# Half of an output projection as seven products of halves, with the weights' sums made by adding DMAs

## The chip, the cores and the metric

The kernel runs on one core of a Trainium2 chip. The metric is the device time of one execution in microseconds. Engines are named as in the profile: PE is TensorE (PEld its weight loads), DVE is VectorE, ACT is ScalarE, POOL is GpSimd and SP is SyncE, which issues most of the DMAs.

## The reference

One layer of a bidirectional encoder on 256 tokens of width 2048, all in float32:

```
x -> x + RMSNorm_post( W_out( sum_b sigmoid(g_b(xn)) * P_b( branch_b(xn) * silu(gate_b(xn)) ) ) )
xn = RMSNorm_pre(x)
```

The branches are a bidirectional gated linear recurrence and a windowed attention with 16 heads. What matters here is the end:

```python
merged = (jax.nn.sigmoid(m_lru) * (y_a @ w_proj_a[l])
          + jax.nn.sigmoid(m_attn) * (y_b @ w_proj_b[l]))
x = x + rms_norm(merged @ w_out[l], norm_post_w[l])
```

`merged` is 256 x 2048 and `w_out` 2048 x 2048. The output projection `merged @ w_out` is the part that the change touches.

## The kernel before

All weights stream through the core once, in the order of a list that `load_plan` writes. Each entry is a load of 1 MiB into a tile `raw` (128 x 2048). A "blk" entry is 128 columns of a matrix over all 2048 rows; a "quad" entry is 512 columns over a quarter of the rows. Two entries after one another for "blk", four for "quad", make one output tile.

The kernel computes in two parts: a float32 operand is split into a rounded high part (type fp32r) and the remainder, and a product is the sum of three matmuls (`mm3`: high by high, high by low, low by high). Weights are split in halves of a load: `split(q)` makes `wh` with a cast on ACT and `wl` with a subtraction on DVE (`parts_of`). The rings are three deep for `raw` and five deep for `wh` and `wl`.

The order of the work is written out by hand. `steps` holds one function for each entry of the plan, and the loop at the end of `body` walks through the half steps `hs`: at the first half of step `i` it issues the load of step `i + 3` on SP (`fetch`); at each half it runs what is due at that half (`due`, filled by `at` and `soon`), then splits the weights for four halves later, then issues the half's matmuls on PE. Each engine runs its own instructions in this order.

The last stages are these. For each of four column blocks `c`, `add_pb` gives `w_proj_b`'s product; its `done` multiplies with the gate and adds the other branch into `sm[c]` (DVE, four operations of 128 x 512). In the two half steps after it, `turn` transposes two blocks of 128 columns on PE into a PSUM bank (`mt`) and splits them into `ms`, the projection's left operand, with tokens in the free dimension. Then comes the projection: for each `c` four quad steps in `add_rows`, 24 matmuls each, 12 in each half, with two PSUM tiles for the tokens 0 to 127 and 128 to 255. `o_evac` squares the result on ACT (`junk`), multiplies it by the norm's weight on DVE (`yw`), and with the last block forms the scale and the output and stores it.

For the last block (`last`) the matmuls of tokens 128 to 255 of its last two steps are held back, so that the first 128 tokens are evacuated and stored beside them.

PSUM has eight banks: tag "bg" has four single banks (`bank`), tag "mm" two pairs (`banks`). The projection's blocks were all taken from "bg" (`spare=True`), one tile for each token block. `load_tail` loads the post norm's weight (`npt`, 2 x 512 KB) and the rows of `x` for the residual (`xr`, 4 x 512 KB) when the projection starts; the tiles come from a pool of 31 units of 4 KB per partition.

Of the kernel before, what the change touches and what calls it, by code (L numbers as in the profile page):

```python
# [27 lines left out]
EPS = 1e-6  # L28
# [14 lines left out]
       ("w_proj_a", 1536), ("w_in", MA0), ("w_in", MA0 + 512)]  # L43


PV_NORM = 0
PV_CW = 16
PV_CB = PV_CW + 64
# [7 lines left out]
def load_plan():  # L56

    plan = []

    def quad(m, c):  # L60
        plan.extend(("quad", m, c, i) for i in range(4))

    def pair(m, c, n):
        plan.extend(("blk", m, c + (n + i) * P, 0) for i in range(2))

    quad("w_in", U0)
    for i in range(8):
# [19 lines left out]
    for c in range(4):  # L87
        quad("w_out", c * 512)
    return plan


def body(ctx, tc, x, xT, wall, wlru, pvec, npost, ident_d, mask_d, rope_d, out):
    nc = tc.nc
# [3 lines left out]
    small = ctx.enter_context(tc.tile_pool(name="small", bufs=2))  # L97
# [3 lines left out]
    def unit(name, dt=F32, shape=(P, 4, S)):  # L101
        return units.tile(list(shape), dt, tag="u", name=name)
# [17 lines left out]
    def parts_of(h, l, src, cast=nc.scalar.copy):  # L120
        cast(h, src)  # L121
        nc.vector.tensor_tensor(l, src, h.bitcast(F32), ALU.subtract)  # L122
# [4 lines left out]
    plan = load_plan()  # L127
# [3 lines left out]
    def at(hs, fn):  # L131
        assert hs >= now[0], (hs, now[0])
        due.setdefault(hs, []).append(fn)
# [7 lines left out]
        at(now[0] + d, fn)  # L141


    raws, parts = {}, {}

    def fetch(i):
        if i >= len(plan) or i in raws:
            return
        raws[i] = ring.tile([P, 2048], F32, tag="raw", name=f"raw{i}", bufs=3)
        nc.sync.dma_start(raws[i], wall[i])  # L150

    def split(q, c=0, w=1024, cast=nc.scalar.copy):
        i, h = q // 2, q % 2
        if i >= len(plan):
            return
        if c == 0:
            parts[q] = [ring.tile([P, 1024], F32R, tag=f"w{s}", name=f"w{s}{i}_{h}", bufs=5) for s in "hl"]
        wh, wl = parts[q]
        parts_of(wh[:, c:c + w], wl[:, c:c + w], raws[i][:, h * 1024 + c:h * 1024 + c + w], cast)

    def mm3(ps, wh, wl, xh, xl, start, stop):
        nc.tensor.matmul(ps, wh, xh, start=start, stop=False)  # L162
# [38 lines left out]
    def add_rows(name, act, done, spare=False, last=False):  # L201


        got, held = [], []

        def products(t, g, h, wh, wl):
            ts = slice(t * P, (t + 1) * P)
            for j in range(2):
                k = 4 * g + 2 * h + j
                sl = slice(j * 512, (j + 1) * 512)  # L210
                a = act[k // 2][:, k % 2, :, ts]
                mm3(got[t], a[:, 0], a[:, 1], wh[:, sl], wl[:, sl], k == 0, k == KT - 1)

        def half(g, h, wh, wl):
            if g == 0 and h == 0:
                if spare:
                    got.extend(bank(f"{name}{t}", (P, 512)) for t in range(2))
                else:
                    ps = banks(name, (P, 2, 512))
                    got.extend(ps[:, t] for t in range(2))  # L220
            products(0, g, h, wh, wl)
            if last and g >= 2:
                held.append((1, g, h, wh, wl))
            else:
                products(1, g, h, wh, wl)
            if g == 3 and h == 1:
                if last:
                    done(0, got[0])
                    for a in held:
                        products(*a)  # L230
                    done(1, got[1])
                else:
                    soon(lambda: [done(t, got[t]) for t in range(2)])

        for g in range(4):
            steps.append(("quad", lambda h, wh, wl, g=g: half(g, h, wh, wl)))


    warm = const.tile([P, 1], F32, name="warm")
# [262 lines left out]
            nc.vector.tensor_tensor(dst, dst, sg, ALU.mult)  # L502
        return done

    tm, sm, ms = [], [], []


    def gate_evac(units_list, c):
# [146 lines left out]
    def add_pb(c):  # L655
        def done(t, ps):
            g = sm[c][:, t]
            nc.vector.tensor_tensor(g, ps, g, ALU.mult)
            nc.vector.tensor_tensor(g, tm[c][:, t], g, ALU.add)
            if t == 1:  # L660
                for i in range(2):
                    soon(lambda i=i: turn(i), i + 1)

        def turn(i):

            ps = bank(f"mt{c}{i}")
            for j in range(2):
                sl = slice((2 * i + j) * P, (2 * i + j + 1) * P)
                for t in range(2):
                    nc.tensor.transpose(ps[:, j, t * P:(t + 1) * P], sm[c][:, t, sl], ident)  # L670
# [25 lines left out]

    def load_tail():
        for h in range(2):
            sl = slice(h * 1024, (h + 1) * 1024)
            npt.append(unit(f"np{h}", F32, (P, 1024)))  # L700
            nc.sync.dma_start(npt[h], npost[:, sl])
            for t in range(2):
                xr[t].append(unit(f"xr{t}{h}", F32, (P, 1024)))
                yw[t].append(unit(f"yw{t}{h}", F32, (P, 1024)))
                nc.sync.dma_start(xr[t][h], x[t * P:(t + 1) * P, sl])

    at(2 * len(steps) + 2, load_tail)

    def o_evac(c):
        def done(t, ps):  # L710
            cs = slice((c % 2) * 512, (c % 2 + 1) * 512)
            junk = small.tile([P, 512], F32, tag="p", name=f"junk{c}{t}", bufs=2)
            sums, bb = so[t], bias[t]
            nc.scalar.activation(junk, ps, AF.Square, accum_out=sums[:, c:c + 1])
            if c == 3:
                nc.scalar.activation(bb, sums[:, 3:4], AF.Sqrt, scale=1.0 / D, bias=bb)
            nc.vector.tensor_tensor(yw[t][c // 2][:, cs], ps, npt[c // 2][:, cs], ALU.mult)
            if c == 2:
                nc.vector.tensor_tensor(sums[:, 0:1], sums[:, 0:1], sums[:, 1:2], ALU.add)
                nc.vector.tensor_tensor(sums[:, 0:1], sums[:, 0:1], sums[:, 2:3], ALU.add)  # L720
                nc.vector.tensor_scalar(bb, sums[:, 0:1], 1.0 / D, EPS, ALU.mult, ALU.add)
                if t == 1:
                    nc.scalar.activation(warm, eps, AF.Sqrt)
            if c == 3:
                nc.vector.reciprocal(bb, bb)
                for q in range(4):
                    cs = slice((q % 2) * 512, (q % 2 + 1) * 512)
                    y = yw[t][q // 2][:, cs]
                    nc.vector.scalar_tensor_tensor(y, y, bb, xr[t][q // 2][:, cs], ALU.mult, ALU.add)
                    eng = nc.sync if q % 2 == 0 else nc.scalar  # L730
                    eng.dma_start(out[t * P:(t + 1) * P, q * 512:(q + 1) * 512], y)
        return done

    for c in range(4):
# [25 lines left out]

def pack_weights(w):
    loads = []
    for kind, m, c, i in load_plan():
        if kind == "quad":
# [58 lines left out]
```

## Time and profile before

| | |
|---|---|
| time, median of 3 runs | 921.52 us (920.87 to 921.70) |
| the profiled execution's own time | 921.43 us |
| its span | 919.6 us |
| granted TensorE clock, mean | 0.998 |
| the projection's matmuls | 384, from 823.8 to 912.2 us of the span |
| DMA in the whole span | 172.30 MB, mean 187 GB/s |

The span runs from the first to the last instruction of the profiled execution; the time has 1.8 us more around it. A row of the groups names the line, the engine, the operation, the tiles written and read, the shape and the count, then the busy time in us and the mean of one in ns, then the engine's idle time just before these instructions and what ended it. A row of the timeline gives start, duration and operation. A row of the windows gives a stretch, its length, and each engine's busy time in it with the number of instructions, then the granted clock, the share of the 16 DMA engines that was busy, and the rate. PE's durations overlap, since matmuls are pipelined.

### The profile page before, as it was taken

How to read it: one execution, taken by the hardware profiler on the slowest of the kernel's cores; microseconds unless marked ns; L12 is line 12 of the kernel's file. 1: busy time of each engine (PE TensorE's matmuls, PEld its weight loads, DVE VectorE, ACT ScalarE, POOL GpSimd, SP SyncE). 2: the span in 40 equal slices, each digit the busy share in tenths (PEclk: the TensorE clock that was granted, in tenths of full speed). 3: DMA queues.
4: the chain of work that ended last, by engine and by line, in shares of the span. 5: the costliest groups of instructions: out<-in, count | busy, mean ns of one | idle time of the engine just before them, and what ended most of it. 6: DMA issues, size and time to landing. Idle time of an engine off the chain costs nothing.

```text
span 919.6 us, 13623 instructions
## 1 busy us (share of the span) xinstructions
PE 910.3 (99%) x5526; PEld 816.2 (89%) x5526; DVE 636.5 (69%) x877; ACT 525.4 (57%) x721; POOL 1.4 (0%) x23
## 2 busy tenths in 40 slices
PE   9999999999999999999999999999999999999996
PEld 8899999999999999888888888888888888888885
DVE  6976858596869788887686869665564555565554
ACT  7678576857487867854554544654464444344451
POOL 0000000000000000000000000000000000000000
PEclk9999999999999999999999999999999999999999
DMA  9765555445455364555444453544555555558532
GB/s 329 261 232 172 178 201 184 165 179 206 144 223 190 137 228 158 183 183 196 176 177 159 163 184 138 184 143 177 183 183 186 184 199 186 205 183 321 184 138 91
DMA packets 27615, 172.30 MB, mean 187 GB/s; under 512 B 3072, under 2 KB 3840, under 8 KB 8480
## 3 DMA queue, kind: packets, MB, share of 16 engines
q1 hardware_dynamic: 26832, 170.27, 52.0%
q10 hardware_dynamic: 720, 1.16, 0.4%
q8 instruction: 43, 0.70, 0.3%
q14 instruction: 20, 0.16, 0.0%
HBM read 169.32 MB, written 2.10 MB: 186 GB/s over the span
## 4 chain that ended last, share of the span: by engine, by line
PE 98%; DMA 1%; DVE 0%; ACT 0%; SPq 0%; DVEq 0%; issue 0%
PE q L186 6%; PE o L164 4%; PE o L162 4%; PE o L163 4%; PE ga L162 3%; PE gl L162 3%; PE gl L164 3%; PE ga L164 3%; PE ga L163 3%; PE gl L163 3%; PE q L185 3%; PE u L162 3%; PE u L164 3%; PE u L163 3%; PE u_ps L349 2%; PE k L162 1%
## 5 line engine op out<-in xcount | busy, mean ns | idle before, releaser
L122 DVE TENSOR_TENSOR wl<-raw,wh 128x1024 fp32r<-128x1024 f32 (+1 forms) x306 | 370.7, 1215 | 224.6 <-ACT wh L121 224.1
L121 ACT CAST wh<-raw 128x1024 fp32r<-128x1024 f32 (+1 forms) x305 | 316.5, 1044 | 239.6 <-PE o L164 33.1
L186 PE MATMUL q<-xs,wh 128*128 128x512 f32 x256 | 89.7, 396 | 0.0
L164 PE MATMUL gl<-xs,wl 128*128 128x256 f32 x256 | 72.5, 283 | 0.0
L164 PE MATMUL ga<-xs,wl 128*128 128x256 f32 x256 | 72.5, 283 | 0.0
L162 PE MATMUL ga<-xs,wh 128*128 128x256 f32 x256 | 72.5, 283 | 0.0
L162 PE MATMUL gl<-xs,wh 128*128 128x256 f32 x256 | 72.4, 283 | 0.0
L163 PE MATMUL gl<-xs,wh 128*128 128x256 f32 x256 | 72.4, 283 | 0.0
L163 PE MATMUL ga<-xs,wh 128*128 128x256 f32 x256 | 72.4, 283 | 0.0
L185 PE MATMUL q<-xs,wl 128*128 128x256 f32 x240 | 67.0, 279 | 0.0
L186 PEld LDWEIGHTS q<-xs,wh 128*128 128x128 f32 x256 | 47.3, 188 | 9.9
L164 PE MATMUL u<-xs,wl 128*128 128x256 f32 x192 | 54.4, 283 | 0.0
L162 PE MATMUL u<-xs,wh 128*128 128x256 f32 x192 | 54.3, 283 | 0.0
L163 PE MATMUL u<-xs,wh 128*128 128x256 f32 x192 | 54.3, 283 | 0.0
L162 PE MATMUL o<-wh,ms 128*128 128x512 f32 x128 | 50.0, 390 | 0.0
L164 PE MATMUL o<-wh,ms 128*128 128x512 f32 x128 | 49.8, 389 | 0.0
L163 PE MATMUL o<-wl,ms 128*128 128x512 f32 x128 | 49.8, 389 | 0.0
L162 PEld LDWEIGHTS gl<-xs,wh 128*128 128x128 f32 x256 | 49.1, 192 | 0.1
L163 PEld LDWEIGHTS gl<-xs,wh 128*128 128x128 f32 x256 | 49.1, 192 | 0.1
L162 PEld LDWEIGHTS ga<-xs,wh 128*128 128x128 f32 x256 | 49.1, 192 | 0.0
L163 PEld LDWEIGHTS ga<-xs,wh 128*128 128x128 f32 x256 | 49.1, 192 | 0.0
L164 PEld LDWEIGHTS ga<-xs,wl 128*128 128x128 f32 x256 | 49.1, 192 | 0.0
(324 smaller groups left out, 2132.8 us busy)
## 6 DMA issues: line engine op xcount, KB each, us to landing
raw<-wall_dram SPq DMA_DIRECT2D x149, 1024.0 KB, 4.8
lraw<-wlru_dram SPq DMA_DIRECT2D x8, 512.0 KB, 5.7
raw<-wall_dram SPq DMA_DIRECT2D x4, 512.0 KB, 7.7
xr<-x_dram SPq DMA_DIRECT2D x4, 512.0 KB, 9.8
raw<-wall_dram SPq DMA_DIRECT2D x4, 256.0 KB, 4.4
xT<-xT_dram SPq DMA_DIRECT2D x4, 256.0 KB, 6.9
np<-npost_dram SPq DMA_DIRECT2D x2, 512.0 KB, 7.7
out_dram<-yw SPq DMA_DIRECT2D x4, 256.0 KB, 2.3
```

The costliest lines, as they stand in the source:

```text
L121: cast(h, src)
L122: nc.vector.tensor_tensor(l, src, h.bitcast(F32), ALU.subtract)
L162: nc.tensor.matmul(ps, wh, xh, start=start, stop=False)
L163: nc.tensor.matmul(ps, wh, xl, start=False, stop=False)
L164: nc.tensor.matmul(ps, wl, xh, start=False, stop=stop)
L185: nc.tensor.matmul(ps[:, 1], wl[:, sl], a[:, 0], start=False, stop=False)
L186: nc.tensor.matmul(ps, wh[:, sl], a, start=k == 0, stop=k == KT - 1)
L349: nc.tensor.matmul(ups[b // 2][:, b % 2, 0], w[:, sl], a[:, m], start=k == 0 and n == 0, stop=k == KT - 1 and n == 2)
```

## The change

Columns 0 to 1023 of the projection are no longer computed block by block. The left operand is cut into four blocks: `a11`, `a12` for tokens 0 to 127 and `a21`, `a22` for tokens 128 to 255, each with the even or the odd 128-row groups of the inner dimension. The weights are cut likewise into four blocks of 1024 rows by 512 columns. Instead of eight block products there are seven (Strassen's, in Winograd's form, with the signs put where the loads need no subtraction). Each product `m1` to `m7` has two "part" steps of 12 matmuls, with a load of 1 MiB each. Columns 1024 to 2047 stay as they were, and their quad steps are laid between the parts, in the order of the string `OUT` (`2.0` is the first quad of block 2, `m1.0` the first part of m1).

Four sums of blocks are needed on the left: `sums_of` makes them in each `turn` from the same PSUM bank (ACT copies `a21`, DVE forms the sums, and ACT and DVE split them). On the right, m2's block is loaded by SP into the ring as before. The other six products use two chains: chain x is loaded with m1's block, and each later product of it adds one more block into the same tiles by a DMA from POOL (m5, m6, m4); chain y is loaded for m3 and added to for m7. Each of these loads is two DMAs of 512 KB. They are issued in the text one step earlier than the ring's loads (`fetch(i + 4, True)`).

`Seven.after` combines the products: ACT copies m1, DVE adds m6, m5, m7 and forms each output block with `o_sum`, which then goes through `o_done`, the former `o_evac`. m5 keeps its PSUM bank until m7 is done. Block 2 still takes two single banks; block 3 takes one pair from "mm", as one tile. The rows of `x` are loaded 36 half steps after the projection's start rather than at it.

```diff
+SEVEN = {
+    "m1": ("a11", "x", (0, 0)),
+    "m2": ("a12", "z", (1, 0)),
+    "m5": ("s1", "x", (0, 1)),
+    "m3": ("s4", "y", (1, 1)),
+    "m6": ("s2", "x", (1, 1)),
+    "m7": ("s3", "y", (0, 1)),
+    "m4": ("a22", "x", (1, 0)),
+}
+OUT = ("2.0 m1.0 m2.0 2.1 m1.1 m2.1 2.2 m5.0 m5.1 2.3 m3.0 m3.1 m6.0 m6.1 3.0 m7.0 m7.1 3.1 m4.0 m4.1 3.2 3.3")
...
+    def fetch(i, ahead=False):
+        if i >= len(plan) or i in raws:
             return
+        if plan[i][0] == "part":
+            m, q = plan[i][3:]
+            chain = SEVEN[m][1]
+            if chain != "z":
+                if (chain, q) not in chains:
+                    chains[chain, q] = unit(f"{chain}{q}a"), unit(f"{chain}{q}b")
+                    add = {}
+                else:
+                    add = {"accum_op": ALU.add}
+                raws[i] = chains[chain, q]
+                for h in range(2):
+                    nc.gpsimd.dma_start(raws[i][h].rearrange("p a b -> p (a b)"), wall[i][:, h * 1024:(h + 1) * 1024], **add)
+                return
+        if ahead:
+            return
...
+    def sums_of(name, src):
+        a = src.rearrange("p a b -> p (a b)")
+        a11, a12, a21 = (a[:, i * P:(i + 1) * P] for i in (0, 2, 1))
+        f = half_unit(f"{name}f", "uu", F32).rearrange("p a (b c) -> p (a b) c", b=2)
+        t = unit(name, F32R, (P, 4, 2, P))
+        ends = src.rearrange("p a (b c) -> p (a b) c", b=2)[:, 0:4:3]
+        nc.scalar.copy(f[:, 3], a21)
+        nc.vector.tensor_tensor(f[:, 0:2], ends, f[:, 3].unsqueeze(1).to_broadcast([P, 2, P]), ALU.subtract)
+        nc.vector.scalar_tensor_tensor(f[:, 2], f[:, 1], -1.0, a11, ALU.mult, ALU.subtract)
+        nc.vector.scalar_tensor_tensor(f[:, 3], f[:, 2], -1.0, a12, ALU.mult, ALU.subtract)
+        parts_of(t[:, :, 0], t[:, :, 1], f)
+        return t
...
+        def half(self, m, q, h, wh, wl):
+            fresh, last = q == 0 and h == 0, q == 1 and h == 1
+            if fresh:
+                self.ps[m] = bank(f"{self.name}{m}", (P, 512))
+            for j in range(2):
+                ah, al = self.rows(SEVEN[m][0], 4 * q + 2 * h + j)
+                sl = slice(j * 512, (j + 1) * 512)
+                mm3(self.ps[m], ah, al, wh[:, sl], wl[:, sl], fresh and j == 0, last and j == 1)
+            if last:
+                soon(lambda: self.after(m))
...
+            elif m == "m6":
+                nc.vector.tensor_tensor(self.u, ps.pop("m6"), self.u, ALU.add)
+                v = self.temp("v")
+                nc.vector.tensor_tensor(v, ps["m5"], self.u, ALU.add)
+                done(0, 1, ps.pop("m3"), v, -1)
...
             parts_of(m[:, :, 0], m[:, :, 1], ps)
+            msum.append(sums_of(f"mx{2 * c + i}", ps))
...
-        add_rows(f"o{c}_", ms, o_evac(c), True, c == 3)
+            add_rows(f"o{c}_", ms, lambda t, ps, c=c: o_done(t, c, ps), c == 2, c == 3)
...
                 fetch(i + 3)
+                fetch(i + 4, True)
```

More of the change, by code (lines that the diff above doesn't have):

```diff
@@ L86, in load_plan @@
             quad("w_in", MA0 + (c + AHEAD) * 512)
-    for c in range(4):
-        quad("w_out", c * 512)
+    for o in OUT.split():
+        a, i = o.split(".")
+        if a in SEVEN:
+            plan.append(("part", "w_out", 0, a, int(i)))
+        else:
+            plan.append(("quad", "w_out", int(a) * 512, int(i)))
     return plan
@@ L158, in split @@
         wh, wl = parts[q]
-        parts_of(wh[:, c:c + w], wl[:, c:c + w], raws[i][:, h * 1024 + c:h * 1024 + c + w], cast)
+        raw = raws[i]
+        if isinstance(raw, tuple):
+            raw = raw[h].rearrange("p a b -> p (a b)")
+        else:
+            raw = raw[:, h * 1024:(h + 1) * 1024]
+        parts_of(wh[:, c:c + w], wl[:, c:c + w], raw[:, c:c + w], cast)
     def mm3(ps, wh, wl, xh, xl, start, stop):
@@ new lines, in body, with __init__, add, rows @@
+    class Seven:
+        def __init__(self, name, act, sums, done):
+            self.name, self.act, self.sums, self.done = name, act, sums, done
+            self.ps = {}
+        def add(self, m, q):
+            steps.append(("part", lambda h, wh, wl: self.half(m, q, h, wh, wl)))
+        def rows(self, a, i):
+            if a[0] == "a":
+                t, b = int(a[1]) - 1, int(a[2]) - 1
+                src = self.act[i][:, b, :, t * P:(t + 1) * P]
+            else:
+                src = self.sums[i][:, SUMS.index(a)]
+            return src[:, 0], src[:, 1]
+        def half(self, m, q, h, wh, wl):
[8 more added lines that the diff above has]
+                soon(lambda: self.after(m))
+        def temp(self, name):
+            return small.tile([P, 512], F32, tag="uu", name=f"{self.name}{name}", bufs=2)
+        def after(self, m):
+            ps, done = self.ps, self.done
+            if m == "m1":
+                self.u = self.temp("u")
+                nc.scalar.copy(self.u, ps.pop("m1"))
+            elif m == "m2":
+                done(0, 0, ps.pop("m2"), self.u, 1)
+            elif m == "m6":
[3 more added lines that the diff above has]
+                done(0, 1, ps.pop("m3"), v, -1)
+            elif m == "m7":
+                nc.vector.tensor_tensor(self.u, ps.pop("m7"), self.u, ALU.add)
+                done(1, 1, ps.pop("m5"), self.u, -1)
+            elif m == "m4":
+                done(1, 0, ps.pop("m4"), self.u, 1)
@@ L503, in silu_evac @@
         return done
-    tm, sm, ms = [], [], []
+    tm, sm, ms, msum = [], [], [], []
     def gate_evac(units_list, c):
@@ L698, in load_tail, with load_rows @@
         for h in range(2):
-            sl = slice(h * 1024, (h + 1) * 1024)
             npt.append(unit(f"np{h}", F32, (P, 1024)))
-            nc.sync.dma_start(npt[h], npost[:, sl])
+            nc.sync.dma_start(npt[h], npost[:, h * 1024:(h + 1) * 1024])
+            for t in range(2):
+                yw[t].append(unit(f"yw{t}{h}", F32, (P, 1024)))
+    def load_rows():
+        for h in range(2):
             for t in range(2):
                 xr[t].append(unit(f"xr{t}{h}", F32, (P, 1024)))
-                yw[t].append(unit(f"yw{t}{h}", F32, (P, 1024)))
-                nc.sync.dma_start(xr[t][h], x[t * P:(t + 1) * P, sl])
+                nc.sync.dma_start(xr[t][h], x[t * P:(t + 1) * P, h * 1024:(h + 1) * 1024])
@@ L707, in body @@
     at(2 * len(steps) + 2, load_tail)
[L709 to L732, printed above, removed]
@@ L734, in body, with o_done @@
-    for c in range(4):
-        add_rows(f"o{c}_", ms, o_evac(c), True, c == 3)
+    at(2 * len(steps) + 36, load_rows)
+    seen = [0, 0]
+    def o_done(t, c, ps):
+        cs = slice((c % 2) * 512, (c % 2 + 1) * 512)
+        junk = small.tile([P, 512], F32, tag="p", name=f"junk{c}{t}", bufs=2)
+        sums, bb = so[t], bias[t]
+        nc.scalar.activation(junk, ps, AF.Square, accum_out=sums[:, c:c + 1])
+        seen[t] += 1
+        if c == 3:
+            assert seen[t] == 4
+            nc.scalar.activation(bb, sums[:, 3:4], AF.Sqrt, scale=1.0 / D, bias=bb)
+        nc.vector.tensor_tensor(yw[t][c // 2][:, cs], ps, npt[c // 2][:, cs], ALU.mult)
+        if seen[t] == 3:
+            nc.vector.tensor_tensor(sums[:, 0:1], sums[:, 0:1], sums[:, 1:2], ALU.add)
+            nc.vector.tensor_tensor(sums[:, 0:1], sums[:, 0:1], sums[:, 2:3], ALU.add)
+            nc.vector.tensor_scalar(bb, sums[:, 0:1], 1.0 / D, EPS, ALU.mult, ALU.add)
+            if seen[1 - t] == 3:
+                nc.scalar.activation(warm, eps, AF.Sqrt)
+        if c == 3:
+            nc.vector.reciprocal(bb, bb)
+            for q in range(4):
+                cs = slice((q % 2) * 512, (q % 2 + 1) * 512)
+                y = yw[t][q // 2][:, cs]
+                nc.vector.scalar_tensor_tensor(y, y, bb, xr[t][q // 2][:, cs], ALU.mult, ALU.add)
+                eng = nc.sync if q % 2 == 0 else nc.scalar
+                eng.dma_start(out[t * P:(t + 1) * P, q * 512:(q + 1) * 512], y)
@@ new lines, in o_sum @@
+    def o_sum(t, c, ps, other, sign):
+        f = small.tile([P, 512], F32, tag="p", name=f"of{t}{c}", bufs=2)
+        nc.vector.scalar_tensor_tensor(f, ps, float(sign), other, ALU.mult, ALU.add if sign > 0 else ALU.subtract)
+        o_done(t, c, f)
+    seven = Seven("o", ms, msum, o_sum)
+    orows = {}
+    for o in OUT.split():
+        a, i = o.split(".")
+        if a in SEVEN:
+            seven.add(a, int(i))
+        elif i == "0":
+            c = int(a)
+            n = len(steps)
+            add_rows(f"o{c}_", ms, lambda t, ps, c=c: o_done(t, c, ps), c == 2, c == 3)
+            orows[a] = steps[n:]
+            steps[n:] = [orows[a].pop(0)]
+        else:
+            steps.append(orows[a].pop(0))
@@ L762, in pack_weights @@
     loads = []
-    for kind, m, c, i in load_plan():
-        if kind == "quad":
+    for kind, m, c, i, *q in load_plan():
+        q = q[0] if q else None
+        if kind == "part":
+            b, f = SEVEN[i][2]
+            f = c + f * 512
+            a = w[m].reshape(2, 4, 2, P, -1)[q, :, b, :, f:f + 512].transpose(1, 0, 2)
+        elif kind == "quad":
             a = w[m].reshape(4, 4, P, -1)[i, :, :, c:c + 512].transpose(1, 0, 2)
```

5 lines of the change are left out of this document (3 added, 2 removed).

## The prediction

> **What bounds the kernel now.** I read the page's head, its chain of work that ended last, and then the last stage alone, because the change touches only the merge and the output projection.
>
> ```profile
> span 919.6 us, 13623 instructions
> PE 910.3 (99%) x5526; PEld 816.2 (89%) x5526; DVE 636.5 (69%) x877; ACT 525.4 (57%) x721; POOL 1.4 (0%) x23
> ...
> PE 98%; DMA 1%; DVE 0%; ACT 0%; SPq 0%; DVEq 0%; issue 0%
> ```
>
> TensorE is busy from end to end and is 98% of the chain, so a matmul taken away is worth its full pace unless something else becomes late. Pool does nothing (1.4 us). The pace is read from the timeline of PE where the projection starts, and from the end of the chain:
>
> ```profile
> 823.62 0.39 PE L164 MATMUL pb__7789<-wh,yb 128*128 128x512 f32 x1
> 823.84 0.39 PE L162 MATMUL o<-wh,ms 128*128 128x512 f32 x1
> 824.07 0.39 PE L163 MATMUL o<-wl,ms 128*128 128x512 f32 x1
> ...
> 826.57 0.82 PE L670 MATMUL mt<-ident,mg 128*128 128x128 f32 x4
> 827.15 0.47 PE L162 MATMUL o<-wh,ms 128*128 128x512 f32 x1
> ...
> 829.99 0.60 PE L670 MATMUL mt<-ident,mg 128*128 128x128 f32 x4
> 830.35 0.48 PE L162 MATMUL o<-wh,ms 128*128 128x512 f32 x1
> ```
> ```profile
> 912.00 0.24 PE o L164
> 912.24 0.02 issue
> 912.26 0.70 ACT junk L714 x2
> ```
>
> A matmul lasts 0.39 us but the next one starts 0.23 us later: they overlap. The 384 matmuls of the projection start between 823.84 and 912.00, with two groups of transposes (0.58 and 0.36 us) among them: (88.16 - 0.94) / 383 = 0.228 us each. So a quad step (24 matmuls) takes 5.47 us and one of the new steps (12 matmuls) 2.73 us. What feeds them:
>
> ```profile
> L122 DVE TENSOR_TENSOR wl<-raw,wh 128x1024 fp32r<-128x1024 f32 x29 | 35.4, 1225 | 33.1 <-ACT wh L121 33.1
> L717 DVE TENSOR_TENSOR yw<-o,np 128x512 f32<-128x512 f32 x7 | 4.8, 688 | 7.8 <-ACT junk L714 7.7
> L122 DVE TENSOR_TENSOR ms<-mt,ms 128x512 fp32r<-128x512 f32 x2 | 1.4, 692 | 1.1 <-ACT ms L121 1.0
> ```
> ```profile
> L121 ACT CAST wh<-raw 128x1024 fp32r<-128x1024 f32 x29 | 30.4, 1052 | 36.4 <-PE o L164 33.1 <-PE pb__7789 L164 3.3
> ```
>
> These are the groups by shape from 822 to 912 us. ACT's cast of a half load waits for PE (33.1 us): PE has to give back a buffer first. The splits are early, and today each has 2.73 us of PE to hide 1.225 us of DVE.
>
> ```profile
> raw<-wall_dram SPq DMA_DIRECT2D x149, 1024.0 KB, 4.8
> ...
> np<-npost_dram SPq DMA_DIRECT2D x2, 512.0 KB, 7.7
> ```
> ```profile
> core 0: us, PE busy (x) PEld busy (x) DVE busy (x) ACT busy (x) POOL busy (x), PEclk, DMA share, GB/s
> 834.00:836.00 2.00, 2.00 (x11) 1.65 (x10) 1.22 (x1) 0.44 (x1) 0.00 (x0) 1.00 1.03 422
> 836.00:838.00 2.00, 2.00 (x11) 1.65 (x10) 0.81 (x1) 1.05 (x1) 0.00 (x0) 1.00 1.04 424
> 823.60:912.00 88.40, 88.39 (x394) 72.83 (x392) 46.35 (x53) 36.63 (x47) 0.00 (x0) 1.00 0.51 187
> ```
>
> In the stretches where the 16 DMA engines are full (share 1.03) they move 420 GB/s: a load of 1 MiB, 1.05 MB, takes 2.5 us of all engines. Of the 4.8 us from issue to landing 2.3 are then latency. Over the whole projection the engines are half used (0.51). This is the reserve on which the change draws.
>
> **The change part by part.** *Matmuls.* Columns 0 to 1023 need 2 x 96 = 192 matmuls; seven products of 24 are 168. 24 fewer at 0.228 us: **-5.5 us**, all of it on the path.
>
> *Rows' sums with the merge.* For each of eight turns ACT gets a 128x128 copy and a 128x512 cast, DVE four operations. Six turns lie behind wide steps with the spare time above: nothing, but some 3 us each if that spare time were gone. The last two stand ahead of the first products. Their PSUM blocks (mt) come from the same four banks as m1, m2 and the two of o2: m2 can start only when the last turn's block has been read by the new sums. The nearest rows:
>
> ```profile
> 826.10 0.69 DVE L659 TENSOR_TENSOR mg<-mg,mg 128x512 f32<-128x512 f32 x1
> 826.71 1.22 DVE L122 TENSOR_TENSOR wl<-raw,wh 128x1024 fp32r<-128x1024 f32 x1
> 828.05 0.69 DVE L122 TENSOR_TENSOR ms<-mt,ms 128x512 fp32r<-128x512 f32 x1
> ```
> ```profile
> L627 DVE TENSOR_TENSOR sg<-o,sg 128x256 f32<-128x256 f32 x16 | 6.7, 416 | 0.0
> ```
> ```profile
> L121 ACT CAST ms<-mt 128x512 fp32r<-128x512 f32 x8 | 4.7, 587 | 16.0 <-PE mt L670 16.0
> L325 ACT ACTIVATE diag<-diag 128x128 f32<-128x128 f32 x2 | 0.6, 311 | 3.8 <-DVE diag L324 3.8
> ```
>
> From 828.74 DVE does 0.42 (128x256) and twice some 0.3 us (128x128, an estimate below the 416 ns row): 829.8. Then ACT's cast 0.59, DVE's rest 0.69 (831.2), ACT's delayed weight cast and DVE's 1.22 (832.7), the second turn's 0.69 + 0.42 + 0.6: 834.5. PE is through m1 at 830.35 + 2.73 = 833.1. **+1.4 us** (0 to 2.5).
>
> *Last quad.* Column 3's two row blocks were two PSUM tiles; now they are halves of one. The held products of rows 128 to 255 then wait, in the changed kernel's order of instructions, for DVE's yw of rows 0 to 127. Before, they ran beside it:
>
> ```profile
> 906.88 0.60 ACT L714 ACTIVATE junk<-o 128x512 f32<-128x512 f32 x1 [7.17 <-PE o L164]
> ```
> ```profile
> 907.60 0.69 DVE L717 TENSOR_TENSOR yw<-o,np 128x512 f32<-128x512 f32 x1 [6.63 <-ACT junk L714]
> ```
>
> The 24 held matmuls began at 912.24 - 5.47 = 906.8; now at 908.3. **+1.5 us** (1.3 to 2).
>
> *Splits and evacuations.* The loads of w_out go from 16 to 22, so 12 more splits: 12 x 1.225 = 14.7 us of DVE, 12.6 of ACT. In the new steps a split of 1.225 us stands against 1.37 us of PE. From m3.0 to m4.1 PE needs 32.8 us, DVE 20 splits (24.5) and nine evacuating operations of about 0.7 (6.3), together 30.8: 94%, with four halves of lead. Taken at 0, bounded in the third rival.
>
> *Loads.* m2 stays on SP; 4 MiB go by Pool as plain loads and 8 MiB as loads that add into the tile. No row shows an adding load, nor a load from Pool. Below, it costs what a load does, 2.5 us per MiB of all engines: one read, one write; it can't be less, since it reads those bytes too. Above, the tile's old bytes are read in a turn of their own and the new ones written in another: three units, 7.5. I take two, 5.0: a load plus a second read of as many bytes, which is the row nearest to it counted twice. The Trainium skill, Collectives: The Full Stack, "The bandwidth ceiling: the fold count and why AG ≠ RS ≠ AR", says that a DMA that adds pays for two source reads, the addition itself being free, and gives 62.28 against 32.35 GB/s, 1.93 times; no run here shows it yet, and by 1.93 the time below would be 1.2 us shorter.
>
> Order matters more than the mean. Pool's queue is in order. m5.1 adds into the chain that holds m1.1 and waits until DVE has split m1.1; behind it wait m3's plain loads, m6, m7 and m4, though m3's tiles are free. From the projection's start DVE has four merges (2.75), two turns (4.8) and six splits (7.35) ahead: 15.1, with hand-overs 16 us. m4.1's first half must have landed for its split (1.05 + 1.22) before PE comes to it, 60 matmuls ahead of the end: 360 x 0.228 + 0.94 + 1.4 - 13.7 - 2.3 = 68.4. So 52.4 us are there for Pool's 7 adding and 2 plain MiB and for SP's 7 (five of weights, two of x). At two units: (14 + 2 + 7) x 2.5 + 2.3 = 59.8, **7.4 us late**, and ACT and DVE stand in order behind the missing tile, so PE waits as long. At one unit 42.3: nothing waits. At three 77.3: 24.9 late. The break is at 1.6 units.
>
> *Sum*: -5.5 + 1.4 + 1.5 + 7.4 = +4.8. The profiled run took 921.43 us (span 919.6 and 1.8 around it), the median of the three timed ones 921.52, so the sum carries over to the median: **926.3 us**. A measurement of this kernel can tell about 0.2%, 1.8 us.
>
> **The rivals.** *1. An adding load costs a load.* The engines are half empty, and they read and write at the same time, so the second read could hide beside the write. Below 1.6 units nothing waits, and -5.5 + 1.4 + 1.5 = -2.6 is left: 918.9, not slower. For it speaks the 0.51; against it that in the full stretches the share is already over 1 with one read per byte. Chance 0.20.
>
> *2. Pool's transfers cost far more than SP's*: three units for the adding ones, or a queue that SP's rows do not show. 24.9 us late, less the 2.6: 943.8. For it speaks that 512 KB pieces already took 7.7 us where whole MiB took 4.8; against it that those six pieces were issued together and queued behind one another. The Trainium skill, DMA: Bandwidth & Descriptors, "Measured (HBM→SBUF, 128 partitions, SWDGE, issued from GpSimd)", gives 6.15 us for 1 MB issued by Pool; with that for all nine, 941.6. No run shows it. Chance 0.20.
>
> *3. DVE becomes the bound* from m3.0 to m4.1, even with loads in time. It is 94% full there; if a sixth of its time went into waits for ACT's casts (before, it waited 33.1 us against 35.4 of work, but then ACT itself waited for PE), it would need 37.0 us, 4.2 more than PE: 923.1. Against it speaks the lead of four halves. Chance 0.10.
>
> **How the numbers follow.** The forecast has 0.50. The range runs from rival 1's 918.9 to rival 2's 943.8: 919 to 944; about 0.08 lies below and 0.12 above. Faster by over 0.2%: most of rival 1, 0.14. Within 0.2%: the rest of it, the low end of the forecast (1.7 units) and half of rival 3, 0.13. Slower: 0.73.
>
> **What would show it.** Right: PE pace unchanged at 0.23 us; in the second half of the projection PE idle for some 7 us in gaps at the halves of m6, m7 and m4, with ACT's wh waiting for a DMA of the tiles x or y; DMA share near 1 from about 840 to 890; one gap of 1 to 2 us at m2 and one before the last 24 matmuls. An adding 512 KB load alone should take about 2 x 1.25 + 2.3 = 4.8 us. Wrong: PE without gaps but for those two (rival 1); DMA share well under 1 while ACT waits for Pool's loads (rival 2, by latency or by Pool); gaps whose releaser is DVE's wl with the tiles long landed (rival 3).

## The result

The changed kernel takes 929.36 us (median of four runs, 928.74 to 929.52); the kernel before took 921.24 us beside it. The ratio is 1.0087 (95% interval 1.0069 to 1.0104): 8.1 us slower, where 4.8 were forecast. The profiled execution of the changed kernel took 928.74 us with a span of 927.0, against 919.6 before: 7.4 us more.

The head of the page, the row of Pool's queue and the shares of the chain, of the kernel after:

```profile
span 927.0 us, 13731 instructions
PE 909.2 (98%) x5502; PEld 812.4 (88%) x5502; DVE 667.2 (72%) x928; ACT 543.1 (59%) x750; POOL 19.8 (2%) x47
q0 software_dynamic: 3456, 12.58, 5.9%
PE 83%; issue 11%; DMA 2%; POOL 2%; DVE 0%; ACT 0%; SPq 0%; DVEq 0%; POOLq 0%; ACTq 0%
```

There are 24 matmuls fewer and yet PE is hardly less busy. The chain, 98% PE before, is 83% PE now and runs in part through Pool and a DMA. Where PE stands still is told by the timeline of PE in the projection; these are its rows with more than 0.2 us of idle time (start, duration, operation, and in brackets the idle time and what ended it):

```profile
835.07 0.47 PE L201 MATMUL om<-wh,ms 128*128 128x512 f32 x1 [1.81 <-DVE mx7f L291]
875.57 0.50 PE L202 MATMUL om<-wl,mx 128*128 128x512 f32 x1 [0.55 <-DVE wl L141]
898.02 0.49 PE L201 MATMUL om<-wh,ms 128*128 128x512 f32 x1 [1.55 <-ACT wh L140]
899.28 0.67 PE L202 MATMUL om<-wl,ms 128*128 128x512 f32 x1 [0.76 <-DVE wl L141]
902.62 0.79 PE L202 MATMUL om<-wl,ms 128*128 128x512 f32 x1 [0.47 <-DVE wl L141]
912.75 0.50 PE L201 MATMUL o__8431<-wh,ms 128*128 128x512 f32 x1 [1.55 <-DVE yw L834]
```

The first row is m2, waiting for the sums of the last turn. The second lies in the second part of m6, behind which block 3 starts at 876.83 us (some of the expectations below call it the gap at m7). The next three are m4's second part. The last is the first of the 24 held products, waiting for yw. The page counts a gap from the modelled end of a matmul, which lies 0.16 us behind the start of the next one (0.39 against 0.23); so each true loss is 0.16 us more: 1.97 us at m2, 1.71 at the held products.

The durations in this list hold a second thing, 0.67 and 0.79 instead of 0.39 to 0.50. The windows show it (PEclk is the third number from the end; the bounds are those at which the granted clock may change, see below):

```profile
896.03:899.45 3.42, 1.10 (x4) 0.37 (x4) 2.17 (x3) 1.66 (x3) 0.00 (x0) 1.00 1.04 289
899.45:902.86 3.41, 2.94 (x7) 1.73 (x8) 1.52 (x2) 2.60 (x3) 0.00 (x0) 0.50 0.07 24
902.86:906.27 3.41, 3.41 (x9) 2.64 (x10) 3.41 (x4) 2.24 (x3) 0.00 (x0) 0.50 0.00 0
906.27:909.69 3.42, 3.42 (x17) 2.81 (x16) 2.60 (x6) 1.93 (x3) 0.00 (x0) 1.00 0.00 0
```

Behind the gap at m4 the clock is granted at a half for 6.8 us: 9 matmuls in 3.41 us where there are 17 at full clock.

The time, put together: -5.5 for 24 matmuls; +1.97 at m2; +1.71 at the held products; +7.5 at m6, m7 and m4. Of this last sum, m6 and m7 have about 1.0 us (0.71 at m6 in the row shown, and 0.3 at m7 in a gap too short for the list). In m4.1, twelve matmuls worth 2.74 us, PE spends from 896.31 us (the last matmul before, 896.08, and its 0.23) to 904.91 us, where block 3 goes on; with the three slow matmuls behind that, 6.5 us are lost. Some 1.8 of them are the half clock alone (eight steps from 902.62 to 906.19 us), since up to 902.62 us PE would have waited for the load in any case. That leaves 5.7 for the late loads themselves. Another 0.6 us lie in gaps under 0.2 us, and the end behind the last matmul is 1.1 us longer: from ACT's last junk to the end of the span it was 7.3 us (912.26 to 919.6), now 8.5 (918.52 to 927.0).

How the load reached PE is in the chain of the kernel after:

```profile
889.00 11.15 DMA x1b<-wall_dram
900.26 1.05 ACT wh L140
901.34 1.24 DVE wl L141
902.62 0.79 PE om L202
```

The last adding load lands at 900.15 us; the prediction's working, 52.4 us + 7.4 behind a start 16 us into the projection, gives 899.6.

### The profile page after: what moved, and what is told of

Same layout as the page of the kernel before. It is cut to its first block, busy times and chain, and to the rows that moved or that the text cites. A ratio compares the mean times of both kernels' runs of the same rounds, so it can differ in the third digit from the quotient of the medians.

```text
span 927.0 us, 13731 instructions
## 1 busy us (share of the span) xinstructions
PE 909.2 (98%) x5502; PEld 812.4 (88%) x5502; DVE 667.2 (72%) x928; ACT 543.1 (59%) x750; POOL 19.8 (2%) x47
## 3 DMA queue, kind: packets, MB, share of 16 engines
q0 software_dynamic: 3456, 12.58, 5.9%
## 4 chain that ended last, share of the span: by engine, by line
PE 83%; issue 11%; DMA 2%; POOL 2%; DVE 0%; ACT 0%; SPq 0%; DVEq 0%; POOLq 0%; ACTq 0%
PE q L225 6%; PE ga L201 3%; PE gl L201 3%; PE ga L203 3%; PE gl L203 3%; PE ga L202 3%; PE gl L202 3%; PE q L224 3%; PE u L201 2%; PE u L203 2%; PE u L202 2%; PE u_ps L459 2%; DMA x1b<-wall_dram 1%; PE k L201 1%; PE k L203 1%
## 5 line engine op out<-in xcount | busy, mean ns | idle before, releaser
L141 DVE TENSOR_TENSOR wl<-raw,wh 128x1024 fp32r<-128x1024 f32 (+1 forms) x294 | 354.8, 1214 | 180.0 <-ACT wh L140 179.4
L140 ACT CAST wh<-raw 128x1024 fp32r<-128x1024 f32 (+1 forms) x293 | 302.5, 1043 | 194.1 <-PE gl L202 22.4
L203 PEld LDWEIGHTS gl<-xs,wl 128*128 128x128 f32 x256 | 49.1, 192 | 0.0
L224 PEld LDWEIGHTS q<-xs,wl 128*128 128x128 f32 x240 | 45.3, 189 | 0.7
L707 ACT ACTIVATE p<-p,nm 128x256 f32<-128x256 f32 x32 | 16.0, 502 | 37.9 <-DVE nm L705 37.9
```

The lines of the kernel that those rows point to most:

```text
L203: nc.tensor.matmul(ps, wl, xh, start=False, stop=stop)
L224: nc.tensor.matmul(ps[:, 1], wl[:, sl], a[:, 0], start=False, stop=False)
L707: nc.scalar.activation(p[:, t], p[:, t], AF.Exp, bias=nm[:, t:t + 1], accum_out=dn[:, t:t + 1])
```

## The experiments

**Is it the adding, or Pool's queue, or DVE?** The loads of m5, m6, m7 and m4, sixteen DMAs of 512 KB (the expectation counts ten), stay where they are, but do not add.

```diff
-                    add = {"accum_op": ALU.add}
+                    add = {}
```

> The ten loads that add into a tile become plain loads into the same tile, on the same queue in the same order; the weights' sums are left out of the result. My theory: an adding load takes about 1.6 times the DMA engines of a plain one, and the late tiles open the gaps at m7 and m4 (about 4.7 us) and, behind them, the stretch at half clock (3.3 us). Both go: 929.4 - 8.0 = 921.4 us, PE without gaps over 0.3 us between m3 and m4, granted clock 1.0 from 896 to 908 us. What stays is the wait of m2 (2.0) and that of the held products (1.7). Rival A, Pool's software queue is slow whatever it carries: the gaps stay, 928 to 930. Rival B, DVE is the bound from m3 to m4: the gaps stay with DVE's wl as releaser, 927 to 930.

Measured: 920.78 us, ratio to the kernel before 0.9996 (0.9987 to 1.0006). Two gaps are left, at m2 and before the held products:

```profile
834.68 0.47 PE L201 MATMUL om<-wh,ms 128*128 128x512 f32 x1 [1.82 <-DVE mx7f L291]
904.50 0.50 PE L201 MATMUL o__8431<-wh,ms 128*128 128x512 f32 x1 [1.55 <-DVE yw L834]
```

The clock stays full to the last matmul. Pool's queue and DVE's work are the same as in the changed kernel, so neither is what delays m6, m7 and m4: the adding is, and with all that follows it costs 8.6 us. The price of one adding load comes from the windows, a stretch of adding loads in the changed kernel, and one of plain loads in this one:

```profile
868.00:880.00 12.00, 11.46 (x50) 9.14 (x50) 8.04 (x8) 6.80 (x7) 4.28 (x5) 1.00 1.06 210
```
```profile
852.00:862.00 10.00, 10.00 (x46) 8.28 (x45) 8.49 (x7) 6.32 (x7) 2.13 (x4) 1.00 1.03 417
```

With the DMA engines full in both (1.06, 1.03), 210 GB/s against 417: the adding load takes 1.99 units. The rate counts each byte of an adding load once, as that of a plain one: Pool's 12 MiB stand in the page's row as 12.58 MB.

**The price by itself.** The kernel before, with loads of 512 KB behind its end.

```diff
+    load(nc.gpsimd, 0)
+    load(nc.gpsimd, 0, **add)
+    for j in range(4):
+        load(nc.gpsimd, j)
+    for j in (3, 0, 1, 2):
+        load(nc.gpsimd, j, **add)
+    for j in (2, 0, 1, 3):
+        load(nc.sync, j)
+    load(nc.sync, 3)
```

> The kernel before, with 512 KB loads behind its end, nothing beside them: on Pool's queue one plain load, one adding load into the same tile, four plain ones together, four adding ones together; then the four plain ones on SP's queue and one more alone. The time of the kernel says nothing here. My theory (an adding load is two units): plain alone 1.25 + 2.3 = 3.6 us from issue to landing, adding alone 4.8; four plain ones move 2 MiB at 420 GB/s in 5 us, four adding ones at 210 GB/s in 10 us; SP's plain ones as Pool's. Rival A: adding costs nothing of its own, both at about 420 GB/s. Rival B: Pool's queue is slower than SP's for plain loads too, 6 us and more for 1 MiB.

Pool's rows of the timeline (the second and the third wait for the load before them to land), and windows inside the four plain loads on Pool, the four adding ones, and SP's plain ones:

```profile
917.26 0.69 POOL L759 DMA_DIRECT2D pr<-wall_dram  x1 [635.59 <-DVE pr L762]
921.68 0.87 POOL L759 DMA_DIRECT2D pr<-wall_dram  x1 [3.73 <-DMA pr<-wall_dram]
927.23 2.20 POOL L759 DMA_DIRECT2D pr<-wall_dram  x4 [4.67 <-DMA pr<-wall_dram]
```
```profile
930.00:935.00 5.00, 0.00 (x0) 0.00 (x0) 0.00 (x0) 0.00 (x0) 0.00 (x0) 0.50 0.90 338
940.00:948.00 8.00, 0.00 (x0) 0.00 (x0) 0.00 (x0) 0.00 (x0) 0.90 (x1) 0.50 1.03 183
953.00:957.00 4.00, 0.00 (x0) 0.00 (x0) 0.00 (x0) 0.00 (x0) 0.00 (x0) 0.50 0.97 387
```

A plain load is waited for until 4.4 us after its issue, an adding one until 5.5: each 0.7 to 0.8 us more than expected, and 1.1 us apart, where 1.25 were expected. Four at a time run at 338 and 183 GB/s, 1.85 times (the plain ones do not quite fill the engines, 0.90), while Pool's plain loads come near to SP's (387). Two units hold; rivals A and B fall.

**What the loads share.** The four plain loads of m3 go into Pool's queue ahead of m5.1's adding ones, which wait for DVE.

```diff
             m, q = plan[i][3:]
+            if (m, q) == ("m5", 1):
+                for n in range(2):
+                    fetch(plan.index(("part", "w_out", 0, "m3", n)))
```

> The four plain 512 KB loads of m3 go into Pool's queue ahead of m5.1's adding loads, into the 15.6 us in which the queue stood. My theory (the order in Pool's queue costs as much as the price of adding): 2 MiB, some 5 us of all DMA engines, leave the backlog behind m5.1, every later adding load lands 4 to 5 us earlier, the gaps at m7 and m4 shrink from 4.7 to under 1 us, and with them goes the stretch at half clock: 921.5 to 923 us; if the half clock has another cause than the gaps, 925. Rival: the adding loads are paced by something else than the engines' total work (each waits for the one before it): then the later ones land no earlier by more than 1 us and the time stays at 928 to 930.

Measured: 923.29 us (921.15 to 925.69), ratio 1.0019 (1.0009 to 1.0029). Pool's rows of the kernel after show what was wasted, the windows what the reordered queue makes of it:

```profile
823.91 0.89 POOL L179 DMA_DIRECT2D x0b<-wall_dram  x1 [1.85 <-DVE wl L141]
840.43 0.87 POOL L179 DMA_DIRECT2D x1a<-wall_dram  x1 [15.63 <-DVE wl L141]
```
```profile
830.00:840.00 10.00, 8.19 (x39) 6.51 (x38) 7.71 (x12) 7.36 (x10) 0.00 (x0) 1.00 0.48 138
```
```profile
830.00:840.00 10.00, 8.22 (x39) 6.55 (x37) 7.71 (x11) 7.28 (x10) 0.48 (x1) 1.00 0.91 345
```

Of ten microseconds in which the DMA engines were half idle (0.48, kernel after), nine are used now (0.91). The last adding load lands at 896.1 us instead of 900.15, 4.0 us earlier, as the chain shows:

```profile
885.08 11.06 DMA x1b<-wall_dram
```

At m4 two gaps of 0.63 and 0.76 us are left, the one at m6 is gone and, in the profiled execution, the clock stays full. 6.1 us come back.

The other way to the same end: x's rows, 2 MiB for the last step, go from SP's queue to the end of Pool's.

```diff
-                nc.sync.dma_start(xr[t][h], x[...
+                nc.gpsimd.dma_start(xr[t][h], x[...
```

> The four 512 KB loads of x's rows (xr) go from SP's queue to the end of Pool's, behind the last adding load. My theory (what delays m4 is the DMA engines' total work, and x's rows share it from 878 to 900 us): 2 MiB, 5 us of all engines, go behind m4's loads; m4's tiles land up to 5 us earlier, the 3.7 us of gaps at m4 go and the half clock with them: 929.4 - 3.7 - 3.3 = 922.4 us, the gap at m7 (0.6 us) stays, and x's rows land by about 902 us, before DVE needs them. Rival: the adding loads are slow by their own chain, whatever lies beside them: no change, 928 to 930.

Measured: 924.12 us, ratio 1.0027 (1.0016 to 1.0038); at m4 one gap of 0.76 us is left, and the one at m6 is gone. The gain of 5.2 us is 1.7 short of the theory. In the profiled execution, 923.82 us, the windows show a loss in another place: here the clock was halved at m2, which it was not in the changed kernel:

```profile
832.84:836.25 3.41, 1.60 (x7) 1.03 (x6) 2.32 (x6) 1.33 (x3) 0.00 (x0) 1.00 0.56 187
836.25:839.66 3.41, 3.41 (x9) 2.64 (x9) 3.15 (x4) 3.35 (x4) 0.00 (x0) 0.50 0.31 130
```

That alone does not explain the 1.7 us, though: three executions of this kernel with a mean granted clock of 0.998, that of the kernel before, took 923.51 to 924.12 us, no less than this one. Without the half clock PE comes earlier to m4 and may wait there instead; no trace shows it, and the cause stays open.

Both edits leave the price of an adding load as it is and take other work out of its way. So the total work of the DMA engines up to m4 sets the lateness, not a chain of one load after the other.

**The held products.** One PSUM tile for each row block of block 3.

```diff
+                elif last:
+                    got.extend(banks(f"{name}{t}", (P, 512)) for t in range(2))
```

> Column block 3 gets one PSUM tile for each of its two row blocks. My theory: the held 24 matmuls no longer wait for DVE's yw of the other rows; the gap of 1.7 to 2.0 us before them goes and nothing later takes its place, since all loads have landed by then: 927.6 us. Rival: the held products meet the next thing that is late (ACT's Square, DVE's work on rows 0 to 127), and less than 0.7 us comes back: 928.7 or more.

Measured: 926.75 us (924.61 to 928.36), ratio 1.0063 (1.0047 to 1.008). The gap before the held products is gone and no other has come. The 2.6 us by the medians are more than the gap of 1.7; the runs differ in the clock, and the profiled one, 924.61 us, had the half clock for one stretch of 3.41 us, not two. Runs of this and of the changed kernel with the same mean granted clock differ by 1.0 us (0.992) and 2.1 us (0.994), which fits the gap. The cause is the single tile, as forecast.

**m2's bank.** Block 2 takes its PSUM from the double banks.

```diff
-            add_rows(f"o{c}_", ms, lambda t, ps, c=c: o_done(t, c, ps), c == 2, c == 3)
+            add_rows(f"o{c}_", ms, lambda t, ps, c=c: o_done(t, c, ps), False, c == 3)
```

> Column block 2 takes its PSUM from the pool of double banks, so that m2 has a bank that no turn of the merge held. My theory: the gap of 1.97 us before m2 goes, but the adding loads start when DVE has split m1.1 and run at their own rate, so PE comes earlier to m7 and m4 and waits there for what it gained: 929 us, no change, the gaps at m7 and m4 in sum 1.5 to 2 us longer. Rival: the loads move forward with PE, and the full 2.0 us comes back: 927.4.

Measured: 928.48 us, ratio 1.0075 (1.006 to 1.009): 0.9 us back, which the two intervals do not tell apart (the changed kernel's is 1.0069 to 1.0104). The theory's place was wrong in part. PE's rows:

```profile
836.34 0.50 PE L201 MATMUL o__8000<-wh,ms 128*128 128x512 f32 x1 [0.60 <-ACT wh L140]
837.59 0.50 PE L202 MATMUL o__8000<-wl,ms 128*128 128x512 f32 x1 [0.76 <-DVE wl L141]
887.71 0.50 PE L202 MATMUL om<-wl,mx 128*128 128x512 f32 x1 [0.57 <-DVE wl L141]
```

m2 starts at once, but the quad behind it stands 1.4 us for its splits (1.8 with what the modelled ends hide), which are behind the rows' sums on ACT and DVE. So little is won at m2 itself, some 0.2 us; Pool's first waiting load starts at 840.18 us instead of 840.43, in a projection that starts 0.24 us earlier, so the adding loads gain nothing; and the gaps where the loads are late are a little longer, by 0.57 us at m7 and 0.21 at m6. Behind the bank there is a second limit: these sums. The next run moves the sums of the last two turns five halves later, besides.

```diff
-            msum.append(sums_of(f"mx{2 * c + i}", ps))
+            add = lambda: msum.append(sums_of(f"mx{2 * c + i}", ps))
+            soon(add, 5) if c == 3 else add()
```

> Two edits to the changed kernel: column block 2 in the double banks, as where m2 got its own bank, and the sums of the last two turns made five halves later. My theory (m2's own bank brought back 0.9 instead of 2.0 us because the splits of the first 15 us stood behind these sums on ACT and DVE): the two short gaps at 836 to 838 us go, m2 starts without a wait, and m1.1's split and with it the adding loads come some 3 us earlier, as in the kernel with all edits, so that the gaps at m7 and m4 shrink by 1 us or more: 929.4 - 2.0 - 1 to 3 = 924.5 to 926.5, 921.5 to 923 if the half clock goes too. Rival: the loads give the gain back at m4, as before: 928 to 929.

Measured: 925.32 us, ratio 1.0047 (1.0029 to 1.0065), as the theory had it. There is no gap before 894 us; m1.1 is split sooner, and Pool's first waiting load starts 5 us earlier than in the kernel after:

```profile
835.47 0.87 POOL L179 DMA_DIRECT2D x1a<-wall_dram  x1 [11.19 <-DVE wl L141]
```

**All of it.** The five edits shown, in one kernel: the order of y's loads, x's rows, two tiles, m2's bank, the later sums.

> All of it together: y's plain loads ahead of m5.1, x's rows behind the last adding load, two PSUM tiles for column block 3, block 2 in the double banks, and the sums of the last two turns made five halves later, so that DVE has the first splits done in time. My theory: the gaps at m2, m7, m4 and before the held products all go; what stays of the change is 24 matmuls less (5.5 us) and a tail 1.1 us longer: 921.4 - 5.5 + 1.1 = 917.0, up to 918.5 if some 0.5 us gaps stay. Rival: as where m2 had its own bank, DVE's and ACT's splits are late in the first 15 us all the same and 1.4 us come back there: 919 to 920. A second: the adding loads still land late at m4: 920 to 923.

Measured: 916.5 us (916.1 to 917.7), ratio to the kernel before 0.995 (0.9937 to 0.9962). It beats both kernels, by 5 us and by 13. PE has no gap over 0.2 us in the projection; its windows (the first numbers behind the comma are PE's busy time):

```profile
823.60:850.00 26.40, 26.40 (x121) 21.60 (x120) 22.07 (x27) 14.94 (x19) 5.22 (x8) 1.00 1.04 328
850.00:880.00 30.00, 30.00 (x134) 24.83 (x133) 24.86 (x28) 19.39 (x25) 9.20 (x11) 1.00 1.04 244
```

The DMA engines are full for 56 us (1.04), and DVE works 47 of them (83%): this is why the order of their work decides, and why DVE itself still does not bind.

**The end of the program.** All loads plain and on SP's queue, none on Pool's.

```diff
-                    add = {"accum_op": ALU.add}
+                    add = {}
...
-                    nc.gpsimd.dma_start(raws[i][h]
+                    (nc.gpsimd if add else nc.sync).dma_start(raws[i][h]
```

> No load goes by Pool and none adds: the weights' sums are left out, all pieces of the three chains are plain 512 KB loads on SP's queue, in the places where Pool issued them. From the last matmul's start to the end of the span the kernel before takes 7.6 us and the changed one 8.7. My theory (the longer end belongs to Pool's queue, on whose completions the end of the program waits too): 7.7 us. Rival: it belongs to the evacuation by the changed functions: 8.5 us or more. The whole: 920 to 921 us, as with plain loads on Pool; if SP's queue, which stands in order behind buffers, delays m2's and the quads' loads, 922 or more.

One profiled execution, 921.83 us, span 920.1. Its chain has ACT's last junk here:

```profile
912.45 0.70 ACT junk L829 x2
```

From there to the end of the span it is 7.65 us; 7.3 before, 8.5 in the changed kernel, 8.4 (910.26 to 918.7) with plain loads on Pool. Against these two, 0.8 us of the longer end goes when Pool loads nothing. But the same stretch is 8.0 us (907.86 to 915.9) with all edits and 7.9 (919.44 to 927.3) with m2's own bank, both with adding loads on Pool: among kernels that load by Pool it differs by 0.6 us. So the theory is not shown; Pool's queue may have a part in it, and what sets the end is open.

**The clock.** In each of these runs the changes of the granted clock lie whole multiples of 3.413 us apart. The pair of windows at m2, with plain loads on Pool (the clock stays) and on SP (it does not):

```profile
832.99:836.40 3.41, 1.72 (x8) 1.46 (x9) 2.06 (x6) 2.10 (x4) 0.00 (x0) 1.00 0.81 291
```
```profile
832.87:836.28 3.41, 1.60 (x8) 1.02 (x7) 2.32 (x6) 1.43 (x3) 0.00 (x0) 1.00 0.63 187
836.28:839.70 3.42, 3.42 (x10) 2.65 (x9) 3.16 (x4) 3.25 (x4) 0.00 (x0) 0.50 1.00 369
```

The gap is the same, 1.8 us, and only its place on the grid differs. To see it alone, the kernel before got 16 pauses, each between two matmuls that add zeros:

```diff
+                z, w = gap["z"], 400 + 100 * (4 * int(name[1]) + g)
+                nc.tensor.matmul(got[0], z[:, 0:P], wh[:, 0:512], start=False, stop=False)
+                for n in range(0, w, 1024):
+                    nc.gpsimd.tensor_copy(z[:, 0:min(1024, w - n)], gap["s"][:, 0:min(1024, w - n)])
+                nc.tensor.matmul(got[0], z[:, 0:P], wh[:, 0:512], start=False, stop=False)
```

> The kernel before with 16 pauses of TensorE in its output projection, one in each quad, between two added matmuls by zeros, while Pool copies 400 to 1900 numbers per partition; each pause is a little longer than the one before, from under 1 to some 3 us, with 5 us of work between them. My theory (from the granted clock of the runs so far): the clock is judged in stretches of 3.41 us on a fixed grid, and goes to half in the next stretch where a little more than half of one was without matmuls; pauses under 1.7 us never do it, those of 1.8 to 3.3 us only where they lie within one stretch, so some do and some do not. Rival: a whole stretch must be idle, so that no pause under 3.4 us has an effect.

The first seven pauses (0.74 to 1.21 us in PE's rows) left the clock alone. Of the nine longer ones (2.13 to 2.91 us) eight were followed by a stretch at half clock. The remaining one, the first of the nine in time, lay across two stretches, 1.9 of its 2.4 us in the earlier. Two windows for each case, that one first:

```profile
876.48:879.89 3.41, 1.51 (x7) 0.93 (x5) 1.93 (x2) 1.04 (x1) 1.70 (x2) 1.00 0.12 50
879.89:883.31 3.42, 2.90 (x13) 2.41 (x14) 0.62 (x2) 0.69 (x2) 0.46 (x1) 1.00 0.57 182
...
886.72:890.13 3.41, 1.04 (x5) 0.87 (x6) 1.36 (x1) 0.73 (x1) 2.24 (x2) 1.00 0.16 24
890.13:893.54 3.41, 3.41 (x10) 2.63 (x9) 0.00 (x0) 0.00 (x0) 0.00 (x0) 0.50 0.70 283
```

The rival, that a whole stretch must be idle, falls: no pause was as long as a stretch.

## Why the prediction was right, and where its steps were not

- *Matmuls, -5.5.* Right: 24 fewer, the pace at full clock unchanged. In the kernel with all edits, where nothing waits, they are nearly the whole difference, 5.0 us; the end behind the last matmul takes 0.7 us back (8.0 against 7.3).
- *m2's bank, +1.4 (0 to 2.5).* Measured 1.97: the turn's sums had read the bank at 834.9 us, forecast 834.5, PE started 0.14 us behind that, and m1 was through at 833.1 us, as forecast. What the step missed is that the same sums also hold back the splits behind them and the start of the adding loads.
- *The held products, +1.5 (1.3 to 2).* Measured 1.71, for the reason given.
- *An adding load, two units.* Right: 1.99 by the rates, 1.85 in the loads alone. The Trainium skill, Collectives: The Full Stack, "The bandwidth ceiling: the fold count and why AG ≠ RS ≠ AR", gives 1.93; the trace agrees. Rival 1 (one unit) is what plain loads did, 920.78 us against its 918.9, without being the case here.
- *Late loads, +7.4.* The start of the waiting load (16 us forecast, 840.43 - 823.76 = 16.7 measured) and the last landing (899.6 and 900.15) were right. The step that was off is the last one: it set the landing of m4.1's second half against the time at which its first half is due. The second half is due 1.37 us later, six matmuls on; and the wait at m2, counted as 1.4, had by then made PE 0.6 us later than that. With the landing 0.55 us later than forecast, 7.4 - 1.37 - 0.57 + 0.55 gives 6.0. The late loads cost 5.7 us with the gaps at m6 and m7, not 7.4.
- *Not foreseen.* The half clock behind the gap, 1.8 us in the profiled execution. It filled just what the step before had too much, so 7.4 and the measured 7.5 at m6, m7 and m4 agree by a cancellation, which is luck. The longer end, 1.1 us, and 0.6 us in short gaps make up most of the difference between +4.8 and +7.4; the rest is 0.6 us at m2 and 0.2 at the held products.
- *Slips that change nothing.* DVE's work ahead of m5.1 adds up to 14.9 us, not 15.1, and was rounded to 16 with the hand-overs. The 912.00 of the last matmul is the chain's piece of it; in PE's timeline it starts at 911.84, and the pace stays 0.23 us.
- *Rival 2* (three units, or a slow software queue) falls with the loads alone. The Trainium skill, DMA: Bandwidth & Descriptors, "Measured (HBM→SBUF, 128 partitions, SWDGE, issued from GpSimd)", gives 6.15 us for 1 MB and, in the same row, 341 GB/s; here four of Pool's plain loads moved 338 GB/s, which agrees with the rate, and 3.1 us for 1.05 MB, which is half the time: the measurement decides.
- *Rival 3* (DVE binds) falls: with all edits DVE is busy 24.86 of 30.00 us from 850 to 880 us, and PE all of them.
- *What ACT and DVE made of a late tile* was as forecast, and one turn further: they stand in order behind it. m4.0's second half was cast late, m7's evacuation stood behind its split, and the cast of m4.1's first half behind that evacuation's junk. This tile had landed at 896.3 us (issued at 884.64, 11.7 us), so standing behind the junk cost it some 0.6 us. ACT's and DVE's rows of the kernel after:

```profile
892.64 1.05 ACT L140 CAST wh<-x0b 128x1024 fp32r<-128x1024 f32 x1 [2.79 <-DMA x0b<-wall_dram]
896.31 0.63 ACT L829 ACTIVATE junk<-of 128x512 f32<-128x512 f32 x1 [2.62 <-DVE of L852]
896.94 1.03 ACT L140 CAST wh<-x1a 128x1024 fp32r<-128x1024 f32 x1
```
```profile
893.73 1.23 DVE L141 TENSOR_TENSOR wl<-x0b,wh 128x1024 fp32r<-128x1024 f32 x1 [2.62 <-ACT wh L140]
895.59 0.69 DVE L852 SCALAR_TENSOR_TENSOR of<-om,ou 128x512 f32<-128x512 f32 x1
```

## What to carry to other kernels

Price a load that adds as two loads of the DMA engines, and ask of the stage, not of the mean, whether they have that time: here 0.51 over the projection looked like room, but for 15.6 us an ordered queue stood behind one split while free loads waited behind it, and putting these ahead gave back 6.1 us. Order such a queue by what can start, and put loads that are needed last behind those that are needed next. Where a change trades matmuls for transfers and sums, look for the small waits it brings (a shared bank, one tile for two halves): here three of them and the order of two queues made 8 us of loss out of 5 us of gain.

## What the runs showed of the hardware

TensorE's granted clock falls to a half after much shorter pauses than I had thought of: it is settled on a fixed grid of 3.41 us, and in the projection a stretch in which PE was busy for 1.62 us or less was followed by one or two at half clock (1.62, 1.60, 1.58, 1.56, 1.10 and 1.04 us are among them), while those with 1.64, 1.72 and 1.81 were not; one stretch with 1.51 us, among the pauses, was spared too, so the bound is not sharp by this measure, whose busy time rests on modelled ends. The Trainium skill, TensorE: Matmul & The Clock Gate, "What's actually happening", has the same free-running window of 3413 ns and the two states, but says that the clock falls after at least one idle window; in these runs a window idle by little more than half was enough. By this a gap of 1.8 us costs PE 1.8 or, by an estimate, some 3.4 us (eight steps of 0.43 instead of 0.23 us follow at m2 with x's rows late), by where it falls on the grid: the same gap at m2 was followed by the half clock in two of the runs shown and not in the others. What of that reaches the time of the kernel depends on the waits behind it. The scatter of the times fits this in part only: of the ten runs with y's loads first the fastest, 921.15 us, had a mean granted clock of 0.997 and the slowest, 925.69 us, one of 0.994, but the one with 0.993 took 924.28 us.
